# Two-layer hybrid decoder step: GpSimd's products move to VectorE, and the merge of the threads gets other prices

## The chip, the core and the metric

The kernel is one launch on one core of a Trainium2 chip. The metric is the device time of that launch in microseconds (us); the kernel before was run three times, and the median counts.

Engine names in the views: PE is TensorE's products, PEld its weight loads, DVE is VectorE, ACT is ScalarE, POOL is GpSimd, SP is SyncE, which issues DMAs.

## The reference, cut to what matters

A group of 2,048 prompt tokens and 64 sample tokens (8 batches of 8) goes through two layers of width 1024 in float32. Layer 0 projects each token to 2,824 columns and runs two branches side by side: a gated delta rule (4 heads, causal convolution of 4 taps on q, k and v, state of 128x128 per head) and sliding-window attention (8 query heads, 2 key heads, window 128, rotary). Layer 1 projects to 4,096 columns and runs a gated linear recurrence with a decay for each feature (HGRN2, 8 heads, state of 128x128):

```
S_t = diag(f_t) S_{t-1} + k_t v_t^T      f = lb + (1 - lb) sigmoid(z)      k = 1 - f
o_t = S_t^T q_t / sqrt(dk)
```

Each layer ends with a gate, an output projection, a residual with layer norm and a gated input of 256 columns per layer:

```
h = layer_norm(ALPHA * x + y, g, b)
out = h + sigmoid(h @ w_ple_gate) * (p @ w_ple_proj)
```

The outputs are the tokens after layer 1 and the new states of both groups.

## The kernel before, in words

**Products.** Each float32 weight and activation of a dense product is split into a high part of 12 bits and the rest, both kept as float32r; a product is then three float32r products per block of 128 rows (`product`, L677). The split takes a copy on ScalarE and a subtraction (`loader`, L630; `xsplit`, L734; `post_loads`, L1919). Everything else on TensorE is float32 or a transposition: products with the states, and many small ones that use only a part of the array, 32 or 64 rows or columns of it.

**Threads and their merge.** The kernel is written as Python generators, one for each piece of work (a tile's attention, a head's delta rule, a head's HGRN unit, the dense products of a layer, the weights' loader). Each yields one instruction at a time. `run` (L512) merges them into one order for each engine: at each step it estimates when each thread's next instruction could start, takes the earliest, and puts it into its engine's queue. All instructions pass through one line of the helper (L351), which is why every row of the views shows that line. The engines then run their queues in this order. What decides the order:

- `op` (L345) gives each instruction a price in ns, by engine, kind and columns. A VectorE `tensor_tensor` of n columns is 1.04 n + 69, a GpSimd one 2.1 n + 148, a float32r product of 256 columns or more n / 2.4 + 2.8.
- `start` (L413) takes the engine's own clock, the ends of the operands' writers and readers, and a table of latencies between engines (`LAT`). A product on the whole array behind one on a part of it gets 40 ns more (`SWITCH`).
- In `run` a product counts as ready only 700 ns after the estimate (`MARGIN`), and the dense thread stands back by 30 ns (`LATER`). So small products of the chains go in when their operands should have been ready for 0.7 us, and dense products fill the rest.
- The estimate holds each engine as its own; it knows nothing of VectorE and GpSimd hindering each other.

**Who does the elementwise work.** Most of it is on VectorE. GpSimd has fixed shares: the six rotary products and sums of an attention tile (`rotary`, L855), the scaling of the probabilities (`att_tile`, L867), the low part of each output (`att_tile`, `rms_out`, L1454, `att_sample`, L1020), two products with the decays in `delta_core` (L1263), the spread of v in `sample_state` (L1564), k's factor in `gates` (L1684) and k's product at each doubling level of `hgrn_core` (L1705). For some others `either` (L612) takes VectorE or GpSimd, whichever clock of the estimate is behind: the low parts of weights (`loader`), of the input (`xsplit`) and of the per-layer input (`post_loads`), the two first products of `hgrn_core`, the last sum of `post_gate` (L1987). GpSimd also does the powers of the norms, memsets, and the DMAs that bring the gated outputs back in `post_loads`.

**Stages.** Layer 0's mixers run to about 1190 us of the profile, its end (`dense_post`, L1868) to about 1600 us, layer 1's mixer to about 2770 us, its end to 3176 us. In an HGRN unit each doubling level multiplies half of q by the decays (`qv`, VectorE), half of k by them (`kv`, GpSimd), forms the next decays (VectorE), and then gives TensorE 4 small products of 32x32 per chunk of 128 tokens.

Of the kernel before, what the change touches and what calls it, by code (L numbers as in the profile page):

```python
# [15 lines left out]
ALU = mybir.AluOpType  # L16
PSUM = bass.MemoryType.PSUM
# [4 lines left out]
NB, NS = 8, 8          # sample: batches, tokens of each  # L22
ST = NB * NS
# [15 lines left out]
# of each layer the parts of the sequence, each in groups of (first tile, prompt tiles, samples too)  # L39
# [4 lines left out]
# the order of layer 0's work in each part: attention of a kv head, delta rule of a head  # L44
# [6 lines left out]
NBLK = 50              # SBUF blocks of 1024 columns  # L51
UNITS = (6, 5, 3)      # at a time, of attention, delta rule and HGRN
XBUDGET = [18, 20]          # blocks of activations at a time
WBUDGET = 14           # blocks of weights at a time
BANKS = 3              # PSUM banks of the dense products
LATER = 30             # ns by which they stand back
MARGIN = 700           # ns that a product waits for the other engines beyond the estimate
SWITCH = 40            # ns from a product on a part of the array to one on the whole
SMALL = (1, 2, 4, 8, 16)     # halves of the blocks inside 32 tokens


def constants():
    """Tables and masks that depend on the shapes alone, packed along the columns."""
# [3 lines left out]
    le = (i[:, None] <= i[None, :]).astype(np.float64)     # [t, i]: t <= i  # L67
    gt = (i[:, None] > i[None, :]).astype(np.float64)      # [t, j]: t > j
# [8 lines left out]
    parts["maskD"] = np.where(le > 0, 0.0, NEG)            # [j, i]  # L77
# [7 lines left out]
    for s in SMALL:  # L85
        # [j, i]: j in the left half of a block of 2 s, i in its right half
        parts[f"m{s}"] = ((j // (2 * s) == c // (2 * s)) & ((j // s) % 2 == 0) & ((c // s) % 2 == 1)).astype(np.float64)
# [8 lines left out]
    # sample: rows (batch of 4, head of 4, token), columns 128 cached keys, then 64 new ones  # L96
# [46 lines left out]
def cut(ap, i):  # L143
    """[p, n] as [p, n / i, i]"""
# [1989 lines left out]
```

## Time and profile before

| | |
|---|---|
| three runs | 3175.2, 3178.25, 3179.35 us; median 3178.25 us |
| span of the profiled execution, first to last instruction | 3176.0 us |
| GpSimd's tensor_tensor, all | 1,145, of which 104 are powers |
| VectorE's tensor_tensor | 1,671 |

The profile has no whole time of the profiled execution beside its span; the span lies inside the range of the three runs. Busy time of an engine is the union of its instructions; a group's mean is that of single instructions, which can overlap. In a group's row, the time behind the second bar is the idle time of the engine just before these instructions, with what ended it. A view of windows gives each engine's busy time in a stretch, and the granted clock of TensorE as a share of its full one.

### The profile page before, as it was taken

To read this page: it belongs to the slowest core of one execution; us is meant where nothing else is said; L and a number is where in the kernel's file an instruction comes from. 1 tells how busy PE (TensorE), PEld (TensorE's weight loads), DVE (VectorE), ACT (ScalarE), POOL (GpSimd) and SP (SyncE) were. 2 spreads that over 40 slices of the span, in tenths; PEclk is the share of its full clock that TensorE was granted. 3 is DMA by queue.
4 is the path that set the end of the run, shared out by engine and by line. 5 is a ranking of instruction groups with operands and counts; after the bars stand their busy time and mean duration, and the time that the engine had idled before them with its cause. 6 is when DMAs were issued, how large, how long until landed. Compare 5 with 4: busy or idle time off the path is not lost. (4 is left out here: it accounts for less than half of the span.)

```text
span 3176.0 us, 64092 instructions
## 1 busy us (share of the span) xinstructions
PE 3054.7 (96%) x25592; PEld 2504.4 (79%) x25592; DVE 1828.4 (58%) x4652; ACT 1146.2 (36%) x3074; POOL 1150.3 (36%) x1306
## 2 busy tenths in 40 slices
PE   8999999999999999999999999999999999899999
PEld 7787877777787778878787878787787877787787
DVE  4467766567767663333457576868566566733332
ACT  4455555555565451111233233334333333311111
POOL 3332234422331352222325354544344344522221
PEclk9989999999999999999999999999999999999999
DMA  4221133321332274345322122122211112644341
GB/s 122 78 72 38 45 90 86 84 57 42 85 91 61 80 189 86 78 89 96 95 65 69 58 66 63 57 62 91 63 52 46 52 51 81 163 99 84 82 85 48
DMA packets 320843, 246.49 MB, mean 78 GB/s; under 512 B 33801, under 2 KB 285841, under 8 KB 320529
## 3 DMA queue, kind: packets, MB, share of 16 engines
q1 hardware_dynamic: 253408, 207.80, 22.4%
q0 software_dynamic: 67136, 34.61, 7.2%
q8 instruction: 201, 3.29, 0.4%
q14 instruction: 98, 0.79, 0.1%
HBM read 182.98 MB, written 60.45 MB: 77 GB/s over the span
## 5 line engine op out<-in xcount | busy, mean ns | idle before, releaser
L351 PE MATMUL bank<-ar,ar 128*128 128x512 f32 (+10 forms) x19788 | 2864.8, 308 | 67.6 <-DVE ar L351 35.7
L351 PEld LDWEIGHTS bank<-ar,ar 128*128 128x128 f32 (+5 forms) x19788 | 2235.7, 164 | 497.0 <-issue 89.5
L351 POOL TENSOR_TENSOR ar<-ar,ar 128x512 f32<-128x512 f32 (+8 forms) x873 | 840.9, 975 | 1592.7 <-ACT ar L351 713.0
L351 ACT ACTIVATE ar<-bank 128x128 f32<-128x128 f32 (+11 forms) x1471 | 530.0, 369 | 1274.7 <-PE bank L351 1155.6
L351 ACT ACTIVATE ar<-ar 128x1024 fp32r<-128x1024 f32 (+12 forms) x828 | 437.1, 549 | 678.1 <-DMA ar<-in_pT 302.4
L351 DVE TENSOR_TENSOR ar<-ar,ar 128x256 f32<-128x256 f32 (+10 forms) x611 | 451.6, 747 | 164.8 <-ACT ar L351 62.0
L351 DVE SCALAR_TENSOR_TENSOR ar<-ar,bank 128x512 f32<-128x512 f32 (+3 forms) x256 | 163.9, 641 | 541.1 <-ACT ar L351 271.3
L351 PE MATMUL bank<-cst,ar 128*128 128x128 f32 (+4 forms) x1439 | 243.6, 278 | 19.7 <-DVE ar L351 14.3
L351 PEld LDWEIGHTS bank<-cst,ar 128*128 128x128 f32 (+4 forms) x1439 | 174.8, 140 | 73.0 <-DVE ar L351 16.4
L351 POOL TENSOR_TENSOR ar<-ar,mhalf 128x1 f32<-128x1 f32 (+3 forms) x104 | 113.1, 1088 | 265.6 <-DVE ar L351 245.4
L351 DVE TENSOR_TENSOR ar<-bank,ar 128x128 fp32r<-128x128 f32 (+8 forms) x326 | 147.4, 455 | 96.6 <-ACT ar L351 68.1
L351 DVE TENSOR_TENSOR ar<-ar 128x32 f32<-128x32 f32 (+11 forms) x452 | 147.0, 334 | 18.6 <-ACT ar L351 15.8
L351 PEld LDWEIGHTS bank<-ar 128*32 128x32 f32 (+3 forms) x3284 | 103.7, 121 | 59.3 <-issue 29.5
L351 PE MATMUL bank<-ar 128*32 128x32 f32 (+4 forms) x3284 | 133.5, 211 | 16.6 <-DVE ar L351 15.0
L351 DVE COPY_PREDICATED ar<-cst,bank 128x128 f32<-128x128 uint32 (+4 forms) x356 | 93.0, 262 | 91.9 <-PE bank L351 81.6
L351 DVE SCALAR_TENSOR_TENSOR ar<-bank,ar,ar 128x509 f32<-128x509 f32 (+8 forms) x216 | 123.6, 573 | 30.7 <-ACT ar L351 27.7
L351 POOL TENSOR_TENSOR ar<-ar 128x40 f32<-128x40 f32 (+7 forms) x156 | 86.2, 561 | 88.8 <-DVE ar L351 37.8
L351 DVE SCALAR_TENSOR_TENSOR ar<-ar,ar,bank 128x128 f32<-128x128 f32 x192 | 65.5, 341 | 79.7 <-PE bank L351 79.3
L351 DVE SCALAR_TENSOR_TENSOR ar<-ar,ar,ar 128x1024 f32<-128x1024 f32 (+1 forms) x68 | 97.1, 1429 | 15.3 <-POOL ar L351 15.2
L351 DVE SCALAR_TENSOR_TENSOR ar<-ar,ar 128x4 f32<-128x4 f32 (+10 forms) x190 | 70.8, 380 | 22.0 <-ACT ar L351 21.0
L351 DVE COPY ar<-ar 32x128 f32<-32x128 f32 (+4 forms) x274 | 68.7, 269 | 4.1 <-POOL ar L351 0.6
L351 ACT ACTIVATION_READ_ACCUMULATOR ar<-bank 128x1 f32 (+1 forms) x340 | 66.2, 195 | 0.1
(58 smaller groups left out, 988.5 us busy)
## 6 DMA issues: line engine op xcount, KB each, us to landing
ar<-os POOLq DMA_DIRECT2D x64, 512.0 KB, 7.5
ar<-in_w_in_odd SPq DMA_DIRECT2D x64, 512.0 KB
ar<-in_w_in_even SPq DMA_DIRECT2D x60, 512.0 KB
os<-ar SPq DMA_DIRECT2D x36, 512.0 KB
ar<-x SPq DMA_DIRECT2D x32, 512.0 KB
os<-ar SPq DMA_DIRECT2D x56, 256.0 KB
ar<-in_x_prompt SPq DMA_DIRECT2D x16, 512.0 KB
ar<-in_w_ple_gate SPq DMA_DIRECT2D x16, 512.0 KB
```

Source lines behind the costliest of these rows:

```text
L351: o.fn = lambda: f(**kw)
```

## The change

It has two parts. First, all of GpSimd's `tensor_tensor` but the powers go to VectorE, and `either` goes away: 1,041 instructions leave GpSimd's queue (1,145 to 104) and enter VectorE's (1,671 to 2,712). GpSimd keeps powers, memsets, four copies and its 68 DMAs. Second, the merge gets other prices: products by size and by the part of the array, 213 ns for a change to the whole array and 100 ns for one to a part, and one more clock, `port`, which instructions of VectorE and GpSimd with two operands in SBUF (and some with one) hold in turn. Number and shapes of the products, of ScalarE's instructions and of the DMAs stay; the helper's line is now L354. The rest of the diff takes comments out.

```diff
-SWITCH = 40
+SWITCH = {True: 213, False: 100}
+STAY = 40
+WHOLE = (128, 128)
...
         if eng == "tensor":
+            lhs = kw["in_"] if m == "transpose" else kw["lhsT"]
+            o.mode = tuple(32 if x <= 32 else 64 if x <= 64 else 128 for x in (lhs.shape[0], lhs.shape[1]))
+            o.place = (lhs.offset // lhs.ap[0][0], out.offset // out.ap[0][0])
+            load = o.mode[1] * 0.84 + 3
             if m == "transpose":
-                o.cost, o.col = n * 0.835 + 2, 128
+                o.cost = max(load, n * 0.835 + 2)
             elif kw["rhs"].dtype == F32R:
-                o.cost, o.col = n / 2.4 + 2.8 if n >= 256 else 216, 128
+                o.cost = max(load, n * 0.4258 + 8)
             else:
-                o.cost = max(n * 4 / 2.4, 54) + 4
-                o.col = out.offset // out.ap[0][0] if sh[0] <= 64 else 128
+                o.cost = max(2 * load, n * 1.74)
...
+        two = sum(hasattr(kw.get(k), "ap") and kw[k].name not in self.bank_key for k in ("in_", "in0", "in1")) - (m == "transpose")
+        o.port = eng == "gpsimd" and m in ("tensor_tensor", "tensor_copy") or eng == "vector" and (two == 2 or two == 1 and m in ("tensor_copy", "tensor_scalar") and out.name not in self.bank_key)
...
-        if eng == "tensor" and o.col == 128 and self.pcol < 128:
-            t += SWITCH       # its weights can't be loaded behind a short product
+        if o.port and self.port > t:
+            t = self.port
+        if eng == "tensor" and o.mode != self.mode:
+            t += SWITCH[o.mode == WHOLE]
...
-            if o.col < 128 and o.col > self.pcol:
-                c = 28        # at the same time as the tile of the array to its left
-            self.pcol = o.col
+            if o.mode == self.mode != WHOLE and o.place != self.place:
+                c = 20 if o.mode[0] == 32 else c / 2 if o.place[1] <= self.place[1] else 14
+            self.mode, self.place = o.mode, o.place
...
+        if o.port:
+            self.port = e
...
                 s = self.start(o, MARGIN if o.eng == "tensor" else 0, True)
+                if o.eng == "tensor" and self.mode != o.mode:
+                    s -= SWITCH[o.mode == WHOLE] - STAY * (o.mode == WHOLE)
...
-    def either(self):
-        return self.V if self.clk["vector"] < self.clk["gpsimd"] else self.G
...
-                    yield self.either().tensor_tensor(out=lv, in0=sv, in1=hv, op=ALU.subtract)
+                    yield self.V.tensor_tensor(out=lv, in0=sv, in1=hv, op=ALU.subtract)
...
-                yield self.G.tensor_tensor(out=kv[:, :, 0, :], in0=kv[:, :, 0, :], in1=bc(bv[:, :, 1], 2, hs), op=ALU.mult)
+                yield self.V.tensor_tensor(out=kv[:, :, 0, :], in0=kv[:, :, 0, :], in1=bc(bv[:, :, 1], 2, hs), op=ALU.mult)
```

The other moved instructions read alike: `self.G` or `self.either()` becomes `self.V` in the functions named above.

**VectorE and GpSimd at two doubling levels of an HGRN unit.** The place is the third head of layer 1, a unit of two chunks, at about 1831 us of the profile before. GpSimd's queue there, before; ar_15795 is k, ar_16807 the decays, the 128x1024 rows are weights being split:

```order
L351 TENSOR_TENSOR ar_17813<-ar_17810,ar_17812 128x1024
L351 MEMSET ar_17520 128x256
L351 TENSOR_TENSOR ar_15795<-ar_15795,ar_16807 128x64x2
L351 TENSOR_TENSOR ar_16807<-ar_16635,ar_16807 128x256
L351 TENSOR_TENSOR ar_17865<-ar_17862,ar_17864 128x1024
L351 TENSOR_TENSOR ar_17449<-ar_17449,ar_15551 128x32
L351 TENSOR_TENSOR ar_15795<-ar_15795,ar_16807 128x32x4
```

VectorE's queue at the same place, before; ar_16635 is q, and the row that has only ar_16807 forms the next decays:

```order
L351 TENSOR_TENSOR ar_16635<-ar_16635,ar_16807 128x64x2
L351 TENSOR_TENSOR ar_16807<-ar_16807 128x64
L351 SCALAR_TENSOR_TENSOR ar_15795<-ar_15795,bank_68 128x256
L351 TENSOR_TENSOR ar_17834<-ar_17831,ar_17833 128x1024
L351 TENSOR_TENSOR ar_15551<-ar_17449 128x64
L351 TENSOR_TENSOR ar_17449<-ar_17449,ar_15551 128x64
L351 COPY_PREDICATED ar_15551<-cst,bank_70 128x64
L351 TENSOR_TENSOR ar_16635<-ar_17449 128x32
L351 TENSOR_TENSOR ar_17449<-ar_17449,ar_15551 128x32
L351 TENSOR_TENSOR ar_16635<-ar_16635,ar_16807 128x32x4
```

VectorE's queue at that step of the same unit after the change; q is ar_16664, k is ar_17248, the decays are ar_17777:

```order
L354 TENSOR_TENSOR ar_16664<-ar_16664,ar_17777 128x64x2
L354 TENSOR_TENSOR ar_16664<-bank_69,ar_17777 128x256
L354 TENSOR_TENSOR ar_17248<-ar_17248,ar_17777 128x64x2
L354 TENSOR_TENSOR ar_17777<-ar_17777 128x64
L354 SCALAR_TENSOR_TENSOR ar_17471<-ar_17471,bank_67 128x256
L354 TENSOR_TENSOR ar_17831<-ar_17828,ar_17830 128x1024
L354 SCALAR_TENSOR_TENSOR ar_17248<-bank_69,nc_109,ar_17248 128x256
L354 COPY_PREDICATED ar_17777<-cst,bank_73 128x64
L354 TENSOR_TENSOR ar_16664<-ar_16664,ar_17777 128x32x4
L354 TENSOR_TENSOR ar_17248<-ar_17248,ar_17777 128x32x4
L354 TENSOR_TENSOR ar_17777<-ar_17777 128x32
L354 TENSOR_TENSOR ar_17871<-ar_17248,ar_17871 128x256
```

The product on k, which was GpSimd's, now stands in VectorE's queue between the one on q and the next decays. Of the weights' subtractions one stands between the two levels, where before two engines had one each.

**TensorE between two levels of that unit.** What stands between the small products of one level and those of the next, before; the 128x512 rows are dense products, and the last row is the next level, 8 products of 32x32 for each chunk:

```order
L351 MATMUL bank_67<-ar_14933,ar_16921 128x512
L351 MATMUL bank_67<-ar_14933,ar_16920 128x512
L351 MATMUL bank_67<-ar_14937,ar_16920 128x512
L351 MATMUL bank_67<-ar_14933,ar_16921 128x512
L351 MATMUL bank_67<-ar_14934,ar_16920 128x512
L351 MATMUL bank_67<-ar_14938,ar_16920 128x512
L351 MATMUL bank_67<-ar_14934,ar_16921 128x512
L351 MATMUL bank_71<-ar_17449 32x32 x2
L351 MATMUL bank_67<-ar_14934,ar_16920 128x512
L351 MATMUL bank_69<-ar_16635,ar_15795 32x32 x8
```

And after the change, at a step of the same unit:

```order
L354 MATMUL bank_68<-ar_14943,ar_16961 128x512
L354 MATMUL bank_68<-ar_14943,ar_16960 128x512
L354 MATMUL bank_68<-ar_14947,ar_16960 128x512
L354 MATMUL bank_68<-ar_14943,ar_16961 128x512
L354 MATMUL bank_68<-ar_14944,ar_16960 128x512
L354 MATMUL bank_68<-ar_14948,ar_16960 128x512
L354 MATMUL bank_68<-ar_14944,ar_16961 128x512
L354 MATMUL bank_69<-ar_17472 32x32 x2
L354 MATMUL bank_68<-ar_14944,ar_16960 128x512
L354 MATMUL bank_73<-ar_16664,ar_17248 32x32 x4
```

The distance is eight dense products in both, and the small products break into the dense ones as often: over TensorE's whole order of 19,344 products the part of the array that is used changes 1,502 times before and 1,497 times after.

More of the change, by code (lines that the diff above doesn't have):

```diff
@@ L167 @@
 class Op:
-    __slots__ = ("eng", "fn", "cost", "rd", "wr", "tab", "nbytes", "col")
+    __slots__ = ("eng", "fn", "cost", "rd", "wr", "tab", "nbytes", "mode", "place", "port")
 class Ask:
@@ L213, in __init__ @@
         self.tab = 0
-        self.pcol = 128
+        self.mode, self.place = WHOLE, None
+        self.port = 0.0
         self.keys = {}
@@ L745, in xsplit @@
             yield self.A.activation(out=h, in_=sv, func=AF.Copy)
-            yield self.either().tensor_tensor(out=l, in0=sv, in1=h, op=ALU.subtract)
+            yield self.V.tensor_tensor(out=l, in0=sv, in1=h, op=ALU.subtract)
             self.free(st)
@@ L974, in att_tile @@
             v = cut(sm[hp], 256)[:, :, lo:]
-            yield self.G.tensor_tensor(out=v, in0=v, in1=bc(den[:, 2 * hp : 2 * hp + 2], 2, 256 - lo), op=ALU.mult)
+            yield self.V.tensor_tensor(out=v, in0=v, in1=bc(den[:, 2 * hp : 2 * hp + 2], 2, 256 - lo), op=ALU.mult)
         pT = [None, None]
@@ L1338, in delta_core @@
         QK = Dm
-        yield self.G.tensor_tensor(out=kT, in0=kT, in1=Gbb, op=ALU.mult)
-        yield self.G.tensor_tensor(out=qT, in0=qT, in1=Gbb, op=ALU.mult)
+        yield self.V.tensor_tensor(out=kT, in0=kT, in1=Gbb, op=ALU.mult)
+        yield self.V.tensor_tensor(out=qT, in0=qT, in1=Gbb, op=ALU.mult)
         self.free(Gbb)
@@ L1478, in rms_out @@
         yield self.A.activation(out=ov[:, 0, :], in_=ob, func=AF.Copy)
-        yield self.G.tensor_tensor(out=ov[:, 1, :], in0=ob, in1=ov[:, 0, :], op=ALU.subtract)
+        yield self.V.tensor_tensor(out=ov[:, 1, :], in0=ob, in1=ov[:, 0, :], op=ALU.subtract)
         self.free(ob)
@@ L1699, in gates @@
         yield self.V.tensor_scalar(out=e1, in0=e1, scalar1=self.lb[:, h : h + 1], scalar2=F_FLOOR, op0=ALU.add, op1=ALU.max)
-        yield self.G.tensor_tensor(out=e2, in0=t, in1=e2, op=ALU.mult)
+        yield self.V.tensor_tensor(out=e2, in0=t, in1=e2, op=ALU.mult)
         self.free(t)
@@ L1941, in post_loads @@
             yield self.A.activation(out=ph, in_=p[:, : 2 * np_], func=AF.Copy)
-            yield self.either().tensor_tensor(out=pl, in0=p[:, : 2 * np_], in1=ph, op=ALU.subtract)
+            yield self.V.tensor_tensor(out=pl, in0=p[:, : 2 * np_], in1=ph, op=ALU.subtract)
             self.free(p)
@@ L1995, in post_gate @@
         self.freebank(pj)
-        yield self.either().tensor_tensor(out=w[:np_], in0=w[:np_], in1=st["x"][:np_, c], op=ALU.add)
+        yield self.V.tensor_tensor(out=w[:np_], in0=w[:np_], in1=st["x"][:np_, c], op=ALU.add)
         if l == 0:
```

18 lines of the change are left out of this document (9 added, 9 removed).

## The prediction

> **What bounds the kernel now.** I read the page's totals, the clock, the stages, TensorE's waits, and then one stretch of waiting in order of time. First the page's line of busy times:
>
> ```profile
> span 3176.0 us, 64092 instructions
> PE 3054.7 (96%) x25592; PEld 2504.4 (79%) x25592; DVE 1828.4 (58%) x4652; ACT 1146.2 (36%) x3074; POOL 1150.3 (36%) x1306
> ```
>
> TensorE is busy for 96% of the span, VectorE and GpSimd for 58% and 36%. A change that leaves TensorE's products as they are can win only what TensorE waits, what its clock loses, and what products cost more in one order than in another. The view of the cores has the granted clock, and the one of the waits (microseconds in total, times, longest) lists who ends TensorE's idle time:
>
> ```profile
> core 0: 3176.0 us, clock 0.985
> ```
>
> ```profile
> PE bank L351 <- DVE ar L351: 76.1, 84, 4.3
> PE bank L351 <- ACT ar L351: 27.1, 21, 7.5
> PE bank L351 <- POOL ar L351: 6.8, 8, 1.6
> PE bank L351 <- DMA ar<-x: 2.5, 2, 1.5
> ```
>
> So 76.1 + 6.8 = 82.9 us end with VectorE or GpSimd, and a clock of 0.985 costs about 0.015 x 3176 = 47.6 us. That is 130 us in reach, 4% of the span. By stages (columns: length, busy time of PE, PEld, DVE, ACT, POOL with counts, clock, DMA share and rate):
>
> ```profile
> core 0: us, PE busy (x) PEld busy (x) DVE busy (x) ACT busy (x) POOL busy (x), PEclk, DMA share, GB/s
> 0.00:1190.00 1190.00, 1128.87 (x11001) 918.65 (x11002) 764.93 (x2283) 645.18 (x1810) 408.63 (x502) 0.97 0.29 81
> 1190.00:1600.00 410.00, 403.99 (x1845) 327.30 (x1843) 135.41 (x215) 56.31 (x114) 107.03 (x93) 1.00 0.44 92
> 1600.00:2770.00 1170.00, 1121.92 (x10929) 933.96 (x10930) 803.82 (x1971) 401.42 (x1073) 534.68 (x620) 0.99 0.23 68
> 2770.00:3176.00 406.00, 399.89 (x1820) 324.45 (x1819) 124.28 (x184) 43.28 (x78) 99.94 (x91) 1.00 0.40 81
> ```
>
> TensorE's idle time and lost clock are in the two mixers (61 and 48 us idle), where the merge interleaves chains with dense products; the ends of the layers have 6 us each. Why the merge misjudges there, the time-ordered view of the HGRN stage shows, VectorE's rows first, then GpSimd's and TensorE's:
>
> ```profile
> 1831.30 2.81 DVE L351 TENSOR_TENSOR ar<-ar,ar 128x1024 fp32r<-128x1024 f32 x1 [0.18 <-ACT ar L351]
> 1836.36 3.15 DVE L351 TENSOR_TENSOR ar<-ar,ar 128x1024 fp32r<-128x1024 f32 x1
> 1830.63 2.39 POOL L351 TENSOR_TENSOR ar<-ar,ar 128x1024 fp32r<-128x1024 f32 x1
> 1836.04 2.40 POOL L351 TENSOR_TENSOR ar<-ar,ar 128x1024 fp32r<-128x1024 f32 x1 [0.22 <-ACT ar L351]
> 1832.15 2.98 PE L351 MATMUL bank<-ar,ar 128*128 128x512 f32 x12
> 1836.12 3.28 PE L351 MATMUL bank<-ar,ar 128*32 128x32 f32 x28 [0.99 <-DVE ar L351]
> 1839.71 0.26 PE L351 MATMUL bank<-ar,cst 128*32 128x32 f32 x4 [0.31 <-DVE ar L351]
> ```
>
> Two VectorE instructions that the merge prices at 1.04 x 1024 + 69 = 1134 ns take 2.81 and 3.15 us beside GpSimd's of the same shape. The chain's next product had been put 0.7 us behind its estimate; its operand is later than that, and TensorE waits 0.99 us with the 28 small products of that row and all dense ones queued behind. Twelve dense products ran just before; some more would have filled the gap.
>
> **The change, part by part.**
>
> *The moved work.* The means on both engines, GpSimd's rows first (the last two are the page's groups), then VectorE's with at most one operand in SBUF:
>
> ```profile
> L351 POOL TENSOR_TENSOR ar<-ar,ar 128x512 f32<-128x512 f32 x180 | 230.6, 1289 | 591.0 <-DVE ar L351 367.0 <-ACT ar L351 106.5 <-PE bank L351 98.3
> L351 POOL TENSOR_TENSOR ar<-ar,ar 128x1024 fp32r<-128x1024 f32 x81 | 200.1, 2471 | 177.0 <-ACT ar L351 162.3 <-DVE ar L351 8.3 <-DMA ar<-in_w_in_even 4.1
> L351 POOL TENSOR_TENSOR ar<-ar,ar 128x256 f32<-128x256 f32 x188 | 149.2, 795 | 224.2 <-PE bank L351 162.6 <-DVE ar L351 42.1 <-ACT ar L351 16.1
> L351 POOL TENSOR_TENSOR ar<-ar,cst 64x1024 f32<-64x1024 f32 x12 | 27.7, 2312 | 1.3 <-ACT ar L351 1.3
> L351 POOL TENSOR_TENSOR ar<-ar,ar 128x512 f32<-128x512 f32 (+8 forms) x873 | 840.9, 975 | 1592.7 <-ACT ar L351 713.0
> L351 POOL TENSOR_TENSOR ar<-ar 128x40 f32<-128x40 f32 (+7 forms) x156 | 86.2, 561 | 88.8 <-DVE ar L351 37.8
> ```
>
> ```profile
> L351 DVE TENSOR_TENSOR ar<-bank,ar 128x256 f32<-128x256 f32 x40 | 16.8, 420 | 11.7 <-POOL ar L351 6.7 <-ACT ar L351 4.6 <-PE bank L351 0.2
> L351 DVE TENSOR_TENSOR ar<-bank,ar 128x512 f32<-128x512 f32 x60 | 41.2, 688 | 20.4 <-POOL ar L351 15.7 <-ACT ar L351 2.5 <-PE bank L351 1.2
> ```
>
> GpSimd's groups hold 873 + 156 + 12 = 1,041 instructions and 840.9 + 86.2 + 27.7 = 954.8 us. An undisturbed VectorE has 420 ns for 256 columns and 688 for 512, so 268 ns for 256 more, and by that slope 688 + 2 x 268 = 1224 for 1024. Against GpSimd's 795, 1289 and 2471 that is 0.53, 0.53 and 0.50. I take 0.53: the move adds 954.8 x 0.53 = 506 us to VectorE.
>
> *The relief.* GpSimd then has only powers, memsets and copies left, so VectorE's instructions with both operands in SBUF should fall to the means of those with one:
>
> ```profile
> L351 DVE TENSOR_TENSOR ar<-ar,ar 128x1024 fp32r<-128x1024 f32 x89 | 145.4, 1635 | 31.0 <-ACT ar L351 29.9 <-issue 0.9
> L351 DVE TENSOR_TENSOR ar<-ar,ar 128x256 f32<-128x256 f32 x227 | 142.6, 633 | 60.6 <-PE bank L351 44.0 <-POOL ar L351 15.0
> ```
>
> These two alone give 89 x (1635 - 1224) = 36.6 and 227 x (633 - 420) = 48.4, together 85 us. VectorE's busy time becomes at most 1828.4 + 506 - 85 = 2249 us (71%); with the other forms relieved too, I expect about 2,100.
>
> *TensorE's waits.* The misjudged waits have one source that both halves of the change remove: contention goes, and what is left of it has a clock in the merge. Bounds: nothing of the 82.9 us goes, or all of it. The excess in the rows above is 1.7 and 2.0 us (2.81 and 3.15 over 1.134), far over the margin of 0.7; without it the 0.99 us would not arise. But 76.1 us in 84 pieces are 0.9 us each, so some will be chains with no dense product in hand, which nothing here cures. I take two thirds: -55 us, nearer to the full end because the row I looked at is of the curable kind. Next late is ScalarE, whose 27.1 us I leave, with the DMA's 2.5.
>
> *The clock.* What lowers it, the windows show, three and a half microseconds each, the first of them with a wait of TensorE in the time-ordered view:
>
> ```profile
> 2043.30:2046.70 3.40, 1.65 (x20) 1.36 (x19) 3.22 (x7) 0.74 (x4) 2.57 (x2) 1.00 0.25 93
> 2046.70:2050.10 3.40, 3.40 (x18) 3.40 (x17) 1.07 (x5) 0.38 (x1) 0.96 (x3) 0.50 0.02 5
> ```
>
> ```profile
> 2045.78 0.32 PE L351 MATMUL bank<-ar,cst 128*32 128x64 f32 x8 [1.75 <-DVE ar L351]
> ```
>
> A stretch of 3.4 us in which TensorE is busy for 1.65 us is followed by one at a clock of 0.50, in which it has no gap at all. At half clock 3.4 us do the work of 1.7, so 47.6 us are some 28 such stretches. Their causes are waits like those above, VectorE and GpSimd both busy in the first row (3.22 and 2.57 of 3.40). If two thirds of the waits go, more than half of these stretches should, but layer 0's start, with a clock of 0.97 in its stage, keeps its own. I take half: -24 us, bounds 0 and -47.6. The Trainium skill, TensorE: Matmul & The Clock Gate, Part 1, says that the clock is halved after at least one idle window of about 3.4 us. By that rule waits of 1.75 us would cost no clock, this term would be nothing and the forecast 24 us later. The rows disagree: the longest wait there is 1.75 us and the clock still falls, so I go by the rows.
>
> *Prices of products and of switches.* The row of the dense products has the mean of one:
>
> ```profile
> L351 PE MATMUL bank<-ar,ar 128*128 128x512 f32 x6624 | 1692.3, 402 | 9.6 <-ACT ar L351 6.0 <-POOL ar L351 2.7 <-DVE ar L351 0.8
> ```
>
> Its price goes from 512 / 2.4 + 2.8 = 216 ns to 512 x 0.4258 + 8 = 226; the x12 row above gives (2.98 - 0.40) / 11 = 235 ns from start to start. What a product really costs does not change by its price, and the order has 1,497 changes of the array's part instead of 1,502. I take 0, bounds -5 and +5.
>
> *New holds on VectorE.* A subtraction for a weight's low part now always stands in VectorE's queue, and VectorE runs it in order; if the weight is late, the chains' products and the emptying of banks are held behind it, and TensorE behind them. GpSimd took 81 of these 170 (81 and 89 in the rows above). How late weights come, the waits show:
>
> ```profile
> ACT ar L351 <- DMA ar<-in_w_in_odd: 50.0, 21, 7.1
> ```
>
> Half of it, 25 us, is the upper bound: had GpSimd's half been on VectorE and each hold passed whole to TensorE. The lower is 0, for the merge places a subtraction behind its copy. I take a third of 25: +8.
>
> *Sum.* 0 - 55 - 24 + 8 = -71 us; 3176.0 - 71 = 3105. The median of the runs is 3178.25, 2.25 above the profiled span, so the forecast is **3107 us**. A measurement here tells about 0.2% (6.4 us) from no change.
>
> **The rivals.**
>
> *A, nothing is gained.* The low price of dense products gave a chain more time than the merge knew: the order shows eight of them between two levels, at 235 - 216 = 19 ns each, 150 ns of slack. The new price takes away 8 x 10 = 80 of it, and the removal of late operands only makes the merge place chains tighter, with waits of the same total. For: a planner that packs always waits where estimates err, and 27.1 us for ScalarE show that it errs without GpSimd. Against: contention's errors of 1.7 us are far larger than 80 ns. Time: 3176 + 0 = 3176 in span, about 3178. Chance 0.15 (0.04 a bit faster, 0.07 the same, 0.04 a bit slower). That the change does not do what it says belongs here: the switch prices change five of 1,502 switches, so they do nothing by their number.
>
> *B, VectorE becomes the bound in the HGRN stage: slower.* There 803.8 + 534.7 x 0.53 = 1087 of 1170 us, 93% without relief. Locally it is over the limit, by the window of 1680 to 1760 and the page's slices of 79.4 us (busy tenths):
>
> ```profile
> 1680.00:1760.00 80.00, 76.53 (x830) 62.32 (x828) 63.44 (x178) 27.27 (x78) 42.76 (x62) 1.00 0.18 52
> ```
>
> ```profile
> DVE  4467766567767663333457576868566566733332
> POOL 3332234422331352222325354544344344522221
> ```
>
> 63.44 + 42.76 x 0.53 = 86.1 us in 80. It decides if less than 6.1 of the 63.44 us is time lost to GpSimd. The stretch's share of the two relieved rows, by GpSimd’s busy time, is 85 x 42.76 / 1150.3 = 3.2 us, not enough by itself; the row 1836.36 (3.15 us for about 1.2) says there is more. In the HGRN stage (the 21st to 35th digit) five slices come to 9.6 tenths or more by digit + 0.53 x digit. If each overruns by 6.1 us, TensorE's queue stands behind VectorE 5 x 6.1 = 31 us more and wins nothing elsewhere: 3178 + 31 = 3209. Chance 0.11.
>
> *C, nearly all of it goes.* The new merge is exact enough that VectorE's waits and with them the low-clock stretches vanish but for 8 us each: -75 - 40 and no holds give 3178 - 115 = 3063. For: with GpSimd's products gone, little is left that makes a VectorE instruction longer than its price. Against: ScalarE's waits and the start's chains stay. Chance 0.14.
>
> **How the numbers follow.** The forecast has 0.60, its own range 3070 to 3150: the terms -55 and -24 each half gone, or each at its far end with no hold. Rival C lies below it, A and B above. 3035 to 3175 leaves out B and about half of A, 0.19. Faster: 0.60 + 0.14 + 0.04 = 0.78; the same 0.07; slower 0.04 + 0.11 = 0.15.
>
> **What would show it.** Right: VectorE's 128x256 products with both operands in SBUF at about 420 ns instead of 633, 128x1024 at about 1.2 us; VectorE busy for 2,100 us; TensorE's waits for VectorE near 30 us with none for GpSimd; a clock of 0.99 or more; dense 128x512 at the mean of 402 ns. Wrong: those waits at 76 us or more (A); long stretches with VectorE at 95% and TensorE waiting for emptied banks (B); a clock that stays at 0.985 with the waits gone, which would put its loss down to something other than waits.

## The result, and the profile after

The changed kernel takes 3147.0 us (median of 4 runs, 3143.56 to 3158.56) against 3176.72 us before: a ratio of 0.9914 with a 95% interval of 0.9895 to 0.9933. It is faster by 30 us, where 71 were forecast, and it lies inside the stated range. The profiled execution has a span of 3146.8 us. First the page's totals, the clock and TensorE's waits of the changed kernel:

```profile
span 3146.8 us, 63372 instructions
PE 3054.1 (97%) x25592; PEld 2507.9 (80%) x25592; DVE 1962.1 (62%) x5693; ACT 1149.5 (37%) x3074; POOL 197.1 (6%) x265
```

```profile
core 0: 3146.8 us, clock 0.983
```

```profile
PE bank L354 <- DVE ar L354: 54.3, 67, 4.8
PE bank L354 <- ACT ar L354: 25.0, 22, 7.7
PE bank L354 <- DMA ar<-x: 4.9, 2, 4.5
```

The moved work itself did what the prediction said. The forms of VectorE, columns as before:

```profile
L354 DVE TENSOR_TENSOR ar<-ar,ar 128x1024 fp32r<-128x1024 f32 x170 | 206.4, 1218 | 58.3 <-ACT ar L354 57.7
L354 DVE TENSOR_TENSOR ar<-ar,ar 128x256 f32<-128x256 f32 x430 | 166.3, 420 | 29.3 <-PE bank L354 26.4
L354 DVE TENSOR_TENSOR ar<-ar,ar 128x512 f32<-128x512 f32 x216 | 146.2, 686 | 3.3
```

The means are 1218, 420 and 686 ns, where 1224, 420 and 688 were expected. GpSimd lost 1150.3 - 197.1 = 953 us and VectorE gained only 1962.1 - 1828.4 = 134. What fell short is on TensorE: its waits for VectorE and GpSimd went from 82.9 to 54.3 us, not to about 30, and its clock from 0.985 to 0.983 instead of up. By stages (cut where layer 0's small products, those on a part of the array, end, where those of HGRN begin, and where they end) the changed kernel has:

```profile
core 0: us, PE busy (x) PEld busy (x) DVE busy (x) ACT busy (x) POOL busy (x), PEclk, DMA share, GB/s
0.00:1169.00 1169.00, 1114.80 (x10916) 909.17 (x10918) 809.01 (x2695) 639.53 (x1798) 33.12 (x64) 0.97 0.28 79
1169.00:1611.00 442.00, 435.24 (x2028) 354.17 (x2029) 188.17 (x316) 70.41 (x146) 48.51 (x46) 0.99 0.39 102
1611.00:2710.00 1099.00, 1075.27 (x10696) 897.15 (x10694) 789.57 (x2413) 384.91 (x1027) 64.24 (x107) 0.99 0.22 65
2710.00:3147.00 437.00, 428.82 (x1959) 347.36 (x1956) 175.34 (x273) 54.62 (x103) 51.26 (x48) 0.99 0.34 88
```

And the kernel before, its first row cut at the same time, its second where its own small products of HGRN begin and end:

```profile
0.00:1169.00 1169.00, 1111.40 (x10938) 905.66 (x10939) 752.26 (x2270) 637.79 (x1801) 395.71 (x495) 0.97 0.29 79
1615.00:2741.00 1126.00, 1081.59 (x10682) 898.61 (x10682) 773.10 (x1912) 382.35 (x1029) 513.93 (x608) 0.99 0.22 65
```

The HGRN stage is 27 us shorter. Layer 0 gained next to nothing: its small products end at 1170 us instead of 1159, HGRN begins at 1611 us instead of 1615, and in the first 1169 us TensorE idles for 54.2 us instead of 57.6, at a clock of 0.97 in both, although GpSimd went from 396 to 33 us there. So the question is where the gain of layer 0 went: taken back by VectorE's longer queue, never there, or eaten by the second half of the change.

### The profile page after: what moved, and what is told of

The parts are those of the page before. It is cut to its first block, busy times and chain, and to the rows that moved or that the text cites. A ratio compares the mean times of both kernels' runs of the same rounds, so it can differ in the third digit from the quotient of the medians.

```text
span 3146.8 us, 63372 instructions
## 1 busy us (share of the span) xinstructions
PE 3054.1 (97%) x25592; PEld 2507.9 (80%) x25592; DVE 1962.1 (62%) x5693; ACT 1149.5 (37%) x3074; POOL 197.1 (6%) x265
## 4 chain that ended last, share of the span: by engine, by line
PE 57%; DVE 7%; DMA 4%; issue 3%; ACT 2%; POOL 0%; SPq 0%; POOLq 0%; DVEq 0%; ACTq 0%
PE bank L354 57%; DVE ar L354 7%; DMA ar<-in_w_in_odd 2%; ACT ar L354 2%; DMA ar<-in_w_in_even 1%; POOL ar L354 0%; SPq L354 0%; DMA ar<-gd 0%; DMA ar<-in_w_ple_gate 0%; DMA ar<-x 0%; DMA os<-ar 0%; ACT L354 0%; DMA ar<-in_w_out_even 0%; DMA ctail<-ar 0%; DMA gd<-ar 0%
## 5 line engine op out<-in xcount | busy, mean ns | idle before, releaser
L354 PE MATMUL bank<-ar,ar 128*128 128x512 f32 (+10 forms) x20168 | 2865.9, 306 | 55.5 <-DVE ar L354 30.8
L354 PEld LDWEIGHTS bank<-ar,ar 128*128 128x128 f32 (+4 forms) x20168 | 2250.9, 163 | 490.4 <-issue 85.8
L354 ACT ACTIVATE ar<-bank 128x128 f32<-128x128 f32 (+13 forms) x1471 | 528.0, 369 | 1343.8 <-PE bank L354 1250.5
L354 DVE TENSOR_TENSOR ar<-ar,ar 128x256 f32<-128x256 f32 (+9 forms) x1517 | 737.1, 514 | 245.2 <-ACT ar L354 207.5
L354 ACT ACTIVATE ar<-ar 128x1024 fp32r<-128x1024 f32 (+12 forms) x833 | 443.1, 551 | 581.7 <-DMA ar<-in_pT 248.6
L354 DVE SCALAR_TENSOR_TENSOR ar<-ar,bank 128x512 f32<-128x512 f32 (+3 forms) x256 | 164.1, 641 | 393.4 <-ACT ar L354 261.6
L354 PE MATMUL bank<-cst,ar 128*128 128x128 f32 (+4 forms) x1439 | 244.2, 280 | 21.1 <-DVE ar L354 14.7
L354 PEld LDWEIGHTS bank<-cst,ar 128*128 128x128 f32 (+4 forms) x1439 | 172.9, 141 | 72.4 <-issue 19.0
L354 DVE TENSOR_TENSOR ar<-bank,ar 128x128 fp32r<-128x128 f32 (+7 forms) x326 | 147.6, 455 | 80.7 <-ACT ar L354 45.2
L354 POOL TENSOR_TENSOR ar<-ar,mhalf 128x2 f32<-128x2 f32 (+3 forms) x104 | 107.6, 1035 | 1361.6 <-DVE ar L354 978.5
L354 DVE TENSOR_TENSOR ar<-ar 128x256 f32<-128x256 f32 (+11 forms) x575 | 135.6, 248 | 15.4 <-ACT ar L354 14.1
L354 DVE SCALAR_TENSOR_TENSOR ar<-bank,ar,ar 128x509 f32<-128x509 f32 (+8 forms) x216 | 123.0, 573 | 26.2 <-ACT ar L354 24.7
L354 DVE COPY_PREDICATED ar<-cst,bank 128x128 f32<-128x128 uint32 (+4 forms) x356 | 93.0, 262 | 72.7 <-PE bank L354 61.5
L354 PEld LDWEIGHTS bank<-ar 128*32 128x32 f32 (+4 forms) x2904 | 90.5, 121 | 45.5 <-DVE ar L354 17.9
L354 PE MATMUL bank<-ar 128*32 128x32 f32 (+5 forms) x2904 | 116.8, 212 | 8.2 <-DVE ar L354 6.9
L354 DVE SCALAR_TENSOR_TENSOR ar<-ar,ar,bank 128x128 f32<-128x128 f32 x192 | 65.7, 342 | 74.1 <-PE bank L354 72.6
L354 POOL MEMSET ar<- 128x256 f32 (+4 forms) x85 | 29.0, 348 | 1141.7 <-PE bank L354 772.8
L354 DVE SCALAR_TENSOR_TENSOR ar<-ar,ar,ar 128x1024 f32<-128x1024 f32 (+1 forms) x68 | 87.0, 1279 | 13.4 <-POOL ar L354 13.3
L354 POOL DMA_DIRECT2D ar<-os x64 | 57.4, 898 | 283.1 <-PE bank L354 214.1
L354 DVE SCALAR_TENSOR_TENSOR ar<-ar,ar 128x512 f32<-128x512 f32 (+10 forms) x187 | 55.9, 304 | 30.4 <-ACT ar L354 29.1
L354 DVE TENSOR_SCALAR ar<-bank 128x512 f32<-128x512 f32 (+2 forms) x80 | 44.6, 592 | 36.2 <-ACT ar L354 35.8
L354 ACT ACTIVATION_READ_ACCUMULATOR ar<-bank 128x1 f32 (+1 forms) x340 | 66.4, 195 | 0.2
```

The costliest lines, as they stand in the source:

```text
L354: o.fn = lambda: f(**kw)
```

## The experiments

All times are medians of 4 to 10 runs, beside runs of the kernel before on the same chip (its medians there: 3177 to 3180 us).

### The halves of the change

**The move alone.** The kernel before, with every moved instruction on VectorE:

```diff
-                    yield self.either().tensor_tensor(out=lv, in0=sv, in1=hv, op=ALU.subtract)
+                    yield self.V.tensor_tensor(out=lv, in0=sv, in1=hv, op=ALU.subtract)
...
-                yield self.G.tensor_tensor(out=kv[:, :, 0, :], in0=kv[:, :, 0, :], in1=bc(bv[:, :, 1], 2, hs), op=ALU.mult)
+                yield self.V.tensor_tensor(out=kv[:, :, 0, :], in0=kv[:, :, 0, :], in1=bc(bv[:, :, 1], 2, hs), op=ALU.mult)
```

> The 1,041 instructions go to VectorE; all prices of the merge stay as before, and no port clock is there. Three theories stand of why 29 us came instead of 71, with the gain in the HGRN stage (its idle time of TensorE fell from 44.4 to 23.7 us) and none in layer 0's mixers (57.6 to 54.2 us idle, clock 0.97 in both). Give-back: contention cost layer 0 as much as HGRN, and VectorE's longer queue there (809 us busy instead of 752) took the relief back. Own turns: layer 0's waits never came from GpSimd, so its relief was worth nothing there. Prices: the new prices of TensorE's products took slack away. Give-back and own turns: the prices are worth nothing, 3140 to 3155 us, waits for VectorE near 54 us. Prices: the move alone is worth the forecast, 3105 to 3125 us.

It takes 3107.2 us, ratio 0.9775 (0.9754 to 0.9797): the whole forecast, from one half of the change. Its totals, clock, waits and two mixers (the rows of the mixers are cut up to 3 us short of their ends):

```profile
span 3101.3 us, 63283 instructions
PE 3031.4 (98%) x25592; PEld 2495.1 (80%) x25592; DVE 1963.9 (63%) x5693; ACT 1150.9 (37%) x3074; POOL 202.2 (7%) x265
```

```profile
core 0: 3101.3 us, clock 0.989
```

```profile
PE bank L351 <- DVE ar L351: 41.3, 50, 5.8
PE bank L351 <- ACT ar L351: 22.1, 26, 7.6
```

```profile
0.00:1125.00 1125.00, 1088.26 (x10887) 890.42 (x10888) 804.50 (x2686) 636.22 (x1789) 32.15 (x62) 0.99 0.30 81
1575.00:2662.00 1087.00, 1072.72 (x10694) 897.58 (x10693) 787.24 (x2411) 382.23 (x1026) 66.60 (x107) 0.99 0.22 65
```

Layer 0's small products end at 1126 us here, some 43 us earlier than in the whole change and 33 earlier than in the kernel before, at about the VectorE load (804.5 us busy) that the whole change has there (809). That ends both theories that blamed layer 0: VectorE's longer queue took nothing back, and the move was worth time there too. The move does two things: it relieves VectorE, and it gives the moved products a faster engine (128x256: a mean of 795 ns on GpSimd before, 420 on VectorE after). No run separates the two, so that relief alone made the gain is not shown.

**The prices alone.** All new prices and the port clock; GpSimd keeps its work:

```diff
-        yield self.V.tensor_tensor(out=e2, in0=t, in1=e2, op=ALU.mult)
+        yield self.G.tensor_tensor(out=e2, in0=t, in1=e2, op=ALU.mult)
...
```

> All new prices and the port clock, but the 1,041 instructions stay where they were. If what cost time was that the merge did not know of the contention, the port clock alone should bring part of the gain: 3150 to 3165 us, waits for VectorE and GpSimd 55 to 70 us. If the lost time of VectorE itself counted, 3170 to 3180 us, waits about 83 us. By the theory of the prices it would be slower than before: over 3185 us.

3206.7 us, ratio 1.0086 (1.0069 to 1.0102), slower, as only the theory of the prices had it. TensorE waits 57.3 us for VectorE, 13.2 for GpSimd and 39.2 for ScalarE, at a clock of 0.979. This kernel has the new prices and the port clock together, so it does not tell what the port clock is worth while GpSimd works: the waits for VectorE and GpSimd did fall, from 82.9 to 70.5 us, and those for ScalarE rose, from 27.1 to 39.2.

**Everything but TensorE's prices.** The move and the port clock, with the old product prices and the old switch:

```diff
-SWITCH = {True: 213, False: 100}
+SWITCH = 40
...
-                o.cost = max(load, n * 0.4258 + 8)
+                o.cost, o.col = n / 2.4 + 2.8 if n >= 256 else 216, 128
```

> The whole change, but with the old prices of TensorE's products and of its switches (216 ns, 40 ns); the port clock stays. Give-back and own turns: 3140 to 3155 us, as the whole change. Prices: 3105 to 3125 us. Its distance to the move alone is what the port clock is worth once GpSimd holds little but powers: I expect under 6 us.

3114.1 us, ratio 0.9794 (0.9776 to 0.9812). So it is TensorE's prices that cost. With the port clock the move is 7 us slower than alone, and the two intervals overlap: with little work left on GpSimd, the port clock brings nothing that shows.

**Layer 0 relieved altogether.** Its moved products are left out:

```diff
-            yield self.V.tensor_tensor(out=v, in0=v, in1=bc(den[:, 2 * hp : 2 * hp + 2], 2, 256 - lo), op=ALU.mult)
...
-        yield self.V.tensor_tensor(out=kT, in0=kT, in1=Gbb, op=ALU.mult)
-        yield self.V.tensor_tensor(out=qT, in0=qT, in1=Gbb, op=ALU.mult)
```

> The whole change, but layer 0's moved products are left out, so that no engine does them: the rotary ones, the scaling of the probabilities, the two products with decays in the delta rule. It lightens VectorE in layer 0 and leaves HGRN as it is. Give-back: TensorE's waits for VectorE in layer 0's mixers fall from 31 us to under 15, its clock there rises over 0.97, and the time is 3125 us or less. Own turns: waits of 24 to 31 us there, the time 3137 to 3150 us.

3143.5 us, ratio 0.9889 (0.9869 to 0.9909); layer 0's small products end at 1163 us instead of 1170, and TensorE's waits for VectorE up to there are 21.3 us instead of 31, in neither range. Less work on VectorE there brings nearly nothing, so under these prices its queue is not the limit of layer 0.

### Which price, and how

Some words that the expectations use from here on: *slack* is the time by which a chain's operand is really ready before TensorE comes to its product; a *turn* is one stretch of dense products with the chain's small products behind it, which costs a pair of switches; the *pick* is the choice of the next instruction, the *booking* the moving on of an engine's estimated clock.

**More margin for the whole change.**

```diff
-MARGIN = 700
+MARGIN = 1050
```

> The whole change with MARGIN at 1050 ns instead of 700. The move alone came to 3107 us, the whole change to 3147, the prices alone to 3207: the new prices of TensorE's products cost 30 to 40 us. Theory slack: the old low prices let TensorE run later than the merge thought, so operands of the chains were ready in real time well before their products; per turn of a chain the new prices book 213 + 100 - 40 = 273 ns for the two switches and about 80 ns for eight dense products, so some 350 ns of hidden margin are gone. Adding 350 ns to the margin should give it back: 3100 to 3120 us, waits of TensorE for VectorE 45 us or less. Rival pick: the new rule takes the switch's 213 or 100 ns off after the operands' margin is counted, so that chains are picked 100 ns too early; then 350 ns also cure it, 3100 to 3120. Rival order: the new prices make another order with other troubles (late loads, pools), which a margin doesn't cure: 3135 to 3160.

3127.5 us, ratio 0.9836 (0.9819 to 0.9853): half of the loss comes back, not all.

**The old price of a switch.**

```diff
-SWITCH = {True: 213, False: 100}
+SWITCH = {True: 40, False: 0}
```

> The whole change with the prices of a switch at 40 and 0 ns instead of 213 and 100; the products' new prices, the port clock and the move stay. Slack: 273 of 350 ns of a turn's slack come back, 3110 to 3122 us. Pick: nothing is taken off any more beside the 40 that stay, all comes back: 3105 to 3117 us. If it were the products' prices and not the switch's: 3140 to 3150 us.

3106.4 us, ratio 0.9775 (0.9749 to 0.9800). Taking this one line back gives the whole 40 us back.

**The old prices of the products**, switches at 213 and 100:

```diff
-                o.cost = max(load, n * 0.4258 + 8)
+                o.cost = n / 2.4 + 2.8 if n >= 256 else 216
...
```

> The whole change with the old prices of the products (216 ns for a dense one of 512 columns instead of 226, and the old ones of float32 and of transpositions); the prices of a switch stay at 213 and 100 ns. Slack: only some 80 of 350 ns come back, 3130 to 3145 us. Pick: nothing comes back, 3140 to 3152 us. If it were the products' prices: 3105 to 3120 us.

3136.7 us, ratio 0.9869 (0.9843 to 0.9896): 10 us faster, inside the range of slack, and the intervals just touch. Against the 3114.1 us with everything of TensorE's prices old, the new price of a switch costs 23 us here, where it costs 41 with the new prices of the products: the two do not add.

**Less margin for the move alone.**

```diff
-MARGIN = 700
+MARGIN = 350
```

> The move alone, all old prices, with MARGIN at 350 ns instead of 700: it takes away about as much slack as the new prices do, without any of them. Slack: 3135 to 3160 us, near the whole change's 3147, with waits of TensorE for VectorE at 50 to 65 us instead of 41 and a clock of 0.98. Pick, or order: the margin of 350 still covers what the merge misjudges without the new rule, 3100 to 3120 us.

3119.0 us, ratio 0.9808 (0.9789 to 0.9828). It costs 12 us and not the 28 to 53 of the expectation: in its simple form, a margin that is short by 350 ns per turn, the theory of slack misses here, and the time lies in the range of its rivals, at its upper end. The waits for VectorE are even lower than in the move alone (29.8 us), those for ScalarE higher (29.0).

**Pick or booking.** The price of a switch acts in the pick of the next instruction, and when TensorE's estimated clock is moved on. First the booking alone:

```diff
-            t += SWITCH[o.mode == WHOLE]
+            t += (STAY if o.mode == WHOLE else 0) if pick else SWITCH[o.mode == WHOLE]
...
-                if o.eng == "tensor" and self.mode != o.mode:
-                    s -= SWITCH[o.mode == WHOLE] - STAY * (o.mode == WHOLE)
```

> The price of a switch alone makes the difference: with 40 and 0 instead of 213 and 100 ns the whole change came to 3106 us. That price works in two places. In the pick it is taken off after the operands' margin has been counted, so that a chain's product on a part of the array is picked with 700 - 100 = 600 ns of margin, one on the whole array with 700 - 173 = 527. In the booking it moves TensorE's clock of the estimate on by 313 ns for a pair of switches instead of 40, which takes slack away. This kernel is the whole change with a pick that takes nothing off the margin (the price of a switch in the pick is 40 or 0, counted before the operands), and books 213 and 100 as the change does. Booking: 3130 to 3150 us. Pick: 3103 to 3117 us.

3157.0 us, ratio 0.9929 (0.9904 to 0.9954), 10 us slower than the whole change and 7 beyond the range of the booking. Then the pick alone:

```diff
+BOOK = {True: 40, False: 0}
...
-            t += SWITCH[o.mode == WHOLE]
+            t += (SWITCH if dm else BOOK)[o.mode == WHOLE]
```

> The counterpart: the whole change, the pick takes 213 and 100 ns off after the margin as the change does, but TensorE's clock of the estimate books 40 and 0 for a switch as before. Booking: 3103 to 3117 us. Pick: 3130 to 3150 us. If each carries half: both kernels at 3120 to 3130 us.

3126.7 us, ratio 0.9836 (0.9820 to 0.9852). Against 3106.4 with neither, the booking costs 51 us and the pick 20; both together cost 41, so they don't add. The booking is the larger part. The first of the two kernels lies beyond every range, the second where each would carry half.

**Half of the price.**

```diff
-SWITCH = {True: 213, False: 100}
+SWITCH = {True: 213, False: 0}
```

> The whole change with 213 ns for a switch to the whole array and 0 for one to a part. Booking: 173 of the 273 ns of slack for a pair stay away, 3128 to 3142 us. Pick: small products on a part have their 700 ns back, products of the chains on the whole array have 527; since the waits of the whole change are half on small products, half on the whole array, 3118 to 3135 us.

3120.5 us, ratio 0.9814 (0.9793 to 0.9835): inside the range of the pick and faster than the booking's lower end of 3128. By itself this run speaks for the pick; that the booking is the larger part rests on the two kernels before it.

**What a margin costs by itself.** The move alone with

```diff
-MARGIN = 700
+MARGIN = 1050
```

> The move alone, all old prices, with MARGIN at 1050 ns instead of 700. With 350 ns more the whole change came to 3127 us and not to 3107. If a margin has a price of its own, because chains that come later make stages end later, this one is slower than the move alone by about as much: 3117 to 3132 us. If it has none, 3100 to 3110 us, and the new prices cost something that no margin gives back.

3125.9 us, ratio 0.9840 (0.9813 to 0.9867). A margin of 1050 costs 19 us where slack is not short. With it the old prices and the new ones give the same time, 3125.9 and 3127.5: that is why the larger margin gave back only half.

### Why a truer price costs time

That the new price of a switch is the truer one, the trace of the changed kernel shows; the numbers are medians from start to start, without idle time between. A dense product of 128x512 follows another after 227 ns. A small one of 32x32 follows a dense one after 327 ns; the dense one behind small ones comes after 121 ns, where 7 lie between the records of small ones; and the next dense one comes after 336. That makes 100 + 114 + 109 = 323 ns for a pair of switches. The change books 313; the old price was 40.

**The same shortage in another place.** Switches stay at 213 and 100; dense products are booked too low instead (512 columns at 203 ns, where the trace has 227):

```diff
-                o.cost = max(load, n * 0.4258 + 8)
+                o.cost = max(load, n * 0.383 + 7)
```

> The whole change with dense products booked about a tenth too low (512 columns at 203 ns instead of 226), switches at their new 213 and 100. The booking of switches at 40 and 0 leaves TensorE's estimated clock short by 1,497 / 2 x 273 ns = 204 us over the kernel; a tenth off the float32r products is about the same 204 us. Theory slack in proportion: it only matters that TensorE's whole booked time is short, by whatever term, so that all other engines run ahead of it in real time: 3103 to 3120 us. Theory place: what matters is the low price at the chain's own switch: 3138 to 3152 us.

3100.7 us, ratio 0.9750 (0.9735 to 0.9765): all of the loss comes back, 2 us below the range of slack in proportion. It has the lowest median of all kernels; the 6 us to the old price of a switch lie within the noise. Its clock, its waits, and one row of the subtractions for weights:

```profile
core 0: 3099.0 us, clock 0.990
```

```profile
PE bank L354 <- DVE ar L354: 34.5, 52, 2.9
PE bank L354 <- ACT ar L354: 20.8, 24, 7.7
PE bank L354 <- DMA ar<-x: 6.1, 2, 5.9
```

```profile
L354 DVE TENSOR_TENSOR ar<-ar,ar 128x1024 fp32r<-128x1024 f32 x170 | 206.9, 1218 | 34.9 <-ACT ar L354 34.5
```

**Everybody else dearer.** TensorE's new prices, the other engines' raised:

```diff
+        if eng in ("vector", "scalar", "gpsimd"):
+            o.cost *= 1.1
```

> The whole change with all its prices of TensorE's products and switches, but every instruction of VectorE, ScalarE and GpSimd priced a tenth higher. The relation of TensorE's booked time to the others' becomes about what it was with the low prices of switches. Slack in proportion: 3103 to 3125 us. Place: 3138 to 3155 us.

3126.0 us, ratio 0.9830 (0.9815 to 0.9846), 1 us past the range of slack in proportion: half of the loss comes back.

**Both shortages.**

```diff
-SWITCH = {True: 213, False: 100}
+SWITCH = {True: 40, False: 0}
...
-                o.cost = max(load, n * 0.4258 + 8)
+                o.cost = max(load, n * 0.383 + 7)
```

> Both low bookings at once: switches at 40 and 0 ns and dense products at 203. If slack is still wanting at 3106 us, 3085 to 3100 us; if it is enough there, 3100 to 3112; if too much slack has a price as the margin of 1050 had (3126 instead of 3107), 3113 to 3130.

3133.0 us, ratio 0.9854 (0.9836 to 0.9873): too much, slower than with either, and beyond my 3130.

**Neither shortage nor margin.** The whole change with

```diff
-MARGIN = 700
+MARGIN = 350
```

> The whole change with MARGIN at 350 ns, so that neither the low bookings nor the margin give slack. Slack: the two stand in for each other, and without both it is much worse than the move alone with 350 (3119): 3165 to 3200 us, slower than the whole change by over 18. If 350 ns of margin cost what they cost with the old prices (12 us): 3150 to 3164 us.

3175.6 us, ratio 0.9997 (0.9981 to 1.0013). Here 350 ns of margin cost 28.6 us, with the old prices 11.8. Margin and low booking stand in for each other.

**Late weights.** The trace of the changed kernel shows a wait that the prediction had as a new hold. Rows of VectorE, ScalarE and TensorE in order of time (start, length, what, and in brackets the idle time before and what ended it):

```profile
1816.24 0.16 DVE L354 TENSOR_TENSOR ar<-ar 128x8 f32<-128x8 f32 x1
...
1818.67 1.06 ACT L354 ACTIVATE ar<-ar 128x1024 fp32r<-128x1024 f32 x1 [3.12 <-DMA ar<-in_w_in_odd]
...
1819.76 1.63 DVE L354 TENSOR_TENSOR ar<-ar,ar 128x1024 fp32r<-128x1024 f32 x3 [3.36 <-ACT ar L354]
...
1821.31 0.15 DVE L354 TENSOR_TENSOR ar<-ar 128x4 f32<-128x4 f32 x1
...
1821.44 0.45 PE L354 MATMUL bank<-ar 128*64 128x64 f32 x4 [1.36 <-DVE ar L354]
```

A weight comes late, ScalarE waits 3.12 us for it, VectorE 3.36 us in front of its subtraction (the first of the x3), and the chain's two products behind that (the other two) reach TensorE 1.36 us late. The same step (the eighth row of its form in the HGRN stage of both) in the kernel with dense products booked low:

```profile
1771.07 0.49 DVE L354 TENSOR_TENSOR ar<-ar,ar 128x128 f32<-128x128 f32 x2 [1.27 <-PE bank L354]
...
1771.48 0.15 DVE L354 TENSOR_TENSOR ar<-ar 128x4 f32<-128x4 f32 x1
1772.46 0.45 PE L354 MATMUL bank<-ar 128*64 128x64 f32 x4
```

No subtraction stands there; VectorE has waited for TensorE, and its result is ready 1772.46 - 1771.56 = 0.90 us early. Over the kernel VectorE idles 58.3 us in front of the 170 subtractions in the changed kernel and 34.9 in this one. So in the next kernel the pick counts what a DMA brings, the weights and every other such operand, as landed 2,500 ns later, and TensorE's prices stay:

```diff
-DMARGIN = 0
+DMARGIN = 2500
```

> The whole change, and the merge counts a weight as landed 2,500 ns after its estimate (the constant for it, DMARGIN, was 0), so that its copy and the subtraction behind it are put later. Theory holds: with TensorE's switches booked in full the estimate lets weights land ahead of time, VectorE stands in front of a subtraction whose weight is late (58.3 us idle ahead of the 170 subtractions, against 36.6 in the move alone and 34.9 with dense products booked short), and the chains' products wait behind it. Then 3110 to 3132 us, and that idle time under 45 us. If the holds are only a side effect: 3138 to 3155 us.

3159.5 us, ratio 0.9939 (0.9919 to 0.9960), 12 us slower than the changed kernel and beyond both ranges:

```profile
L354 DVE TENSOR_TENSOR ar<-ar,ar 128x1024 fp32r<-128x1024 f32 x170 | 206.2, 1219 | 44.5 <-ACT ar L354 43.4 <-DMA ar<-in_w_in_even 0.5
```

```profile
PE bank L354 <- DVE ar L354: 52.3, 76, 2.7
```

The idle time ahead of the subtractions fell as expected, to 44.5 us, and TensorE's waits for VectorE hardly moved, from 54.3 to 52.3 us. The holds are real, but with some of them gone these waits are no shorter. The same margin for weights in the fastest kernel:

> The fastest so far (the whole change with dense products booked at 203 ns, 3101 us) with the same 2,500 ns for weights. If late weights still hold VectorE there, 3088 to 3097 us; if the short booking has already given them their time, 3098 to 3106; if the weights come so late that dense products stand, over 3106.

3128.9 us, ratio 0.9842 (0.9823 to 0.9862), 28 us slower, the third and worst of its cases. Here too the idle time ahead of the subtractions fell, from 34.9 to 22.8 us, and TensorE's waits for VectorE did not, 34.5 to 41.5 us. Since this margin costs 28 us in a kernel that misses no slack, the times of the two kernels do not tell what the holds are worth; that they are not the main cause rests on the waits alone.

**By stages.** The ends of layer 0's small products and the length of the HGRN stage, from one trace of each kernel, in us, with its clock and the median time:

| kernel | layer 0 ends | HGRN | clock | median |
|---|---|---|---|---|
| before | 1159 | 1126 | 0.985 | 3177 to 3180 |
| the change | 1170 | 1099 | 0.983 | 3147.0 |
| the move alone | 1126 | 1090 | 0.989 | 3107.2 |
| change, switch 40 / 0 | 1124 | 1091 | 0.990 | 3106.4 |
| change, dense 203 | 1125 | 1091 | 0.990 | 3100.7 |
| change, margin 350 | 1185 | 1105 | 0.984 | 3175.6 |
| move alone, margin 1050 | 1130 | 1106 | 0.984 | 3125.9 |
| change, switch 40 / 0 and dense 203 | 1125 | 1110 | 0.982 | 3133.0 |

Missing slack is paid mostly in layer 0 (1126 to 1170, to 1185 with half of the margin gone too), and surplus slack in the HGRN stage (1090 to 1106 and 1110) while layer 0 stays at 1124 to 1130. The move alone lies between too little and too much.

## Why the prediction was wrong, point by point

- **The move's price and relief: right, relief too low.** The means came out within 6 ns. VectorE's busy time of 1962 us lies under the 2,100 expected: with 506 us of new work the relief was 1828 + 506 - 1962 = 372 us, where the 2,100 had 234 in it, 85 of them from two forms. The 372 rest on the estimate of 506; the last section has a second way, which gives 300.
- **Waits and clock: right for the move alone.** There the waits for VectorE and GpSimd fell from 82.9 to 41.3 us, holds included; -55 + 8 = -47 was forecast and -42 came. The clock's loss fell from 47.6 to 0.011 x 3101.3 = 34.1, which is -13.5 instead of -24. ScalarE's and the DMA's waits gave 27.1 - 22.1 + 2.5 = 7.5 more. The span fell by 74.7 us where 71 was forecast: these terms make 63 of it, and 12 us are in none of them. Some 10 of the 12 are busy time of TensorE, which fell by 3054.7 - 3031.4 = 23.3 us, 13.5 of them by the clock; the prediction put nothing there. So part of the agreement is errors that cancel.
- **The failed step: "What a product really costs does not change by its price ... I take 0, bounds -5 and +5."** The first half holds: 128x512 has a mean of 401 ns against 402. But the price sets the order, and by the four combinations of the move and the prices (with the port clock) it costs 3147.0 - 3107.2 = 40 us with the move and 3206.7 - 3178.8 = 28 without. I counted changes of the array's part, 1,502 and 1,497, and not what booking them at 313 ns a pair instead of 40 does to the estimate. With both halves together the waits for VectorE and GpSimd fell by 28.6 us instead of 55, and the clock's loss went from 47.6 to 0.017 x 3146.8 = 53.5 us instead of down by 24. That the time lies inside the range even so is luck: its upper part stood for half of either term, not for a loss by the prices.
- **Rival A had the mechanism and the wrong size.** It said that low prices gave chains time which the merge did not know of, and then counted only the dense products, 80 ns a turn, and let it cancel the whole gain. The switch's 273 ns were left out. Nor is it a sum in ns per turn: 350 ns of margin cost 12 us in one kernel and 29 in the other.
- **Rival B did not happen.** VectorE is busy for 789.57 of 1099 us in the HGRN stage, 72% and not 93%, and no slice of the page there has more than 8 tenths. **Rival C**, nearly all waits gone, did not happen either.
- **The clock's rule.** "Wrong: a clock that stays at 0.985 with the waits gone" was not put to the test, for the waits were not gone. The move alone, with 3101.3 - 3031.4 = 69.9 us of idle time, has a clock of 0.989, the change, with 92.7, one of 0.983. But the kernel before, with 121.3 us, has 0.985: the sum of the idle time does not set the clock, and half of the waits gone need not bring half of the loss back. What the falls follow stands in the last section.

Shown is that the move brings 72 us with the old prices, that with the other new prices in place the new price of a switch takes 40 back, that about as much shortage in the dense products' price (some 200 us over the kernel) gives it back, and that margin and shortage stand in for each other in part. That the way is slack is argued from these runs: its sums in ns missed at several of them. Not settled is through which queue the missing slack reaches TensorE: with fewer late weights in front of VectorE, TensorE's waits for it stayed as they were. Why surplus slack lengthens the HGRN stage is not settled either; that its chains, put later, then bound the stage is only argued.

## What to carry to other kernels

When a planner merges queues by estimates, its errors are part of the tuning: here a bottleneck engine that was priced too low seems to have given all others a lead in real time, and a truer price took that away. So a change to a price is costed by how far it moves the bottleneck's estimated clock against the others' (here about 1,497 / 2 x 273 = 204 us), not by whether it is truer; and margin and price are tuned again together. When a change has two halves, each is given its own term with both signs, since here one brought 72 us and the other took 40.

## What the runs showed of the hardware that was not expected

Work that kept GpSimd busy for 953 us lengthened VectorE's busy time by only 134 us: on VectorE alone it would have been 506 by the estimate in the prediction, and so by estimate 372 us of VectorE's own time had been lost while both engines ran. By the durations of single instructions, which can overlap, it is less: all of VectorE's add up to 2042 us before and 2259 after, and the moved ones make some 517 at their new means, which leaves 300. The form of 128x1024 went from 1635 to 1218 ns, that of 128x256 from 633 to 420, with the work that GpSimd had done beside them gone.

When TensorE's clock falls, the traces of all 20 kernels show together. The clock changes at steps of 3.41 us, as at 2046.70 and 2050.10 in the kernel before. Take the idle time of TensorE in each such step at full clock, from 60 us on. Of 136 steps with 1.8 us of idle time or more, 134 are followed by one at half clock; of 17,055 steps with less than 1.0 us, 52 are. In 45 of the 134 no single wait in the step was as long as 1.7 us, and in only 13 was one over 3.0. So a little over half a step of idle time was enough, in one wait or in several, and idle time spread thinly cost hardly any clock. This bears the prediction's reading of its rows out, and it is why the clock does not follow the sum.
